# Expert blocks of layer 0 in groups of four, with more tokens gathered, in a two-block transformer kernel

## The chip, the cores and the metric

The kernel runs on one core of a Trainium2 chip, as one program of 61176 instructions in the profiled execution. The metric is the device time of one execution in microseconds (us), the median of several. Before the change three runs took 4265.05, 4275.7 and 4276.56 us, so the median is 4275.7.

## The reference, cut to what matters

The program is two transformer blocks on one sequence. The first block has two layers; each ends with `peer_ffn`, a feed-forward network that picks 128 of 16384 experts for every token (8 heads of 16), each expert a row of `expert_u` and a row of `expert_v`:

```python
D_MODEL, SEQ, CTX_LEN, N_EXPERTS = 1024, 256, 256, 128 * 128

def peer_ffn(h, w_query, sub_keys, expert_u, expert_v):
    ...
    idx = ...    # per token 8 heads x 16 experts
    gate = ...   # their softmax weights
    def block(args):
        tb, ib, gb = args
        act = jax.nn.gelu(jnp.einsum('pkd,pd->pk', expert_u[ib], tb), approximate=False) * gb
        return jnp.einsum('pk,pkd->pd', act, expert_v[ib])
    ...

for i in range(2):              # first block
    ...                         # mixer of layer i: gated delta rule, then windowed attention
    x = x + g2 * peer_ffn(modulate(x, norm2_g[i], sh2, sc2), ...)
    if i == 0:                  # the 256 context tokens go through layer 0 as well
        xc = xc + cg2 * peer_ffn(modulate(xc, norm2_g[i], csh2, csc2), ...)
...                             # second block: mixers, cross attention, mixture of experts
```

So the network of layer 0 sees 512 tokens (256 of the sequence and 256 of the context), that of layer 1 sees 256. The second block ends in a mixture of experts whose weights fill the last third of the profile. All numbers are float32.

## The kernel before, in words

`peer` (line 926) is the network of one layer; `l` is the layer and `n` the number of tokens, T = 256 in layer 1 and T2 = 512 in layer 0. Nearly all of its numbers stand in tables by `n` at lines 38 to 58. `x = FEW[n]` tokens, the last of the 512, take one way, the other `nd = n - x` tokens another. In layer 0, x is 96 and nd 416; in layer 1, x is 0.

**The way of the nd tokens: all experts, masked.** The 16384 experts are 128 blocks of 128. `up(b)` (line 942) computes one block's activations for all nd tokens: the block's u rows come from DRAM (two blocks per transfer of 1 MB into a tile `w`, a ring of three that all weight loads of the program share), are split into a high and a low part of the fp32r type (`wsplit`: ACT writes `whi`, line 347, DVE or POOL writes `wlo`, line 348), and meet the tokens, split in the same way, in 8 x 3 matmuls of nd columns (`mm3`, lines 517 to 519, tile `hps`). ACT applies the gelu into `h`. Then the activations are multiplied with the gate matrix of the block, which is zero where a token didn't pick an expert, split again (`ahi`, `alo`), and multiplied with the block's v rows, 8 x 3 matmuls (tile `dps`, one PSUM bank for each 128 of the 1024 output columns), whose result is scaled by the modulation and added to X, the residual, in SBUF.

The loop (line 1032) takes two blocks a pass, so each PSUM sum covers two blocks, and DVE adds it to X in two instructions (`add`, line 1026, 256 and 160 columns); when no more u blocks are left, one of the 8 adds goes over ACT and POOL (`OFF`). The activations are computed `AHEAD` passes before they are used: 17 in layer 0, in a ring of 18 tiles `hst` of two blocks. 24 further blocks (`SPILL` 12) are computed early too and wait in DRAM (`hd`). The early blocks fill places where TensorE would wait for other engines: 15 (`HEAD`) in the tail of `route`, which picks the experts, the others among the gate matrices.

**The gate matrices** (lines 977 to 1007). For each token two matmuls of one-hot matrices (`oh`, written by DVE, four operations for eight tokens) give the 128 x 128 matrix of its gates (tile `pg`), ACT copies it to a stage, and for each 32 tokens a tile of 2 MB goes to DRAM (`gd`); the loop reads it back by blocks (`gt`). The generator `side`, parts of layer 1's modulation with weights of their own, is stepped in `route` and once in 16 tokens here.

**The way of the x tokens: gathered rows.** `few` (line 1120) is a generator; one step is two tokens. For each token POOL issues two indirect DMAs of 512 KB (line 1134), which fetch the token's 128 u rows (`gu`) and v rows (`gv`), one pair ahead (`LEAD`), from three buffers for u and three for v (`GB`). TensorE broadcasts the token's row to all partitions, in two halves of 512 columns (line 1155, a PSUM tile `bc` each; `few_rows` has cut the row into three bf16 parts), DVE multiplies and sums each half (line 1156), ACT applies the gelu, DVE the gates (`z`), and four fp32 matmuls of 32 result rows (line 1166) sum the v rows into `dn`, which collects 64 tokens before it is transposed (line 1175) and added to X. `tick` (line 1018) steps the generator: each call adds `RATE` to a count, and every 64 make one pair. It is called after each half of the v matmuls, from the fourth pass on (`FIRST`), and after each `up`.

**What sets the order.** A list scheduler of the tile framework puts the instructions of each engine in order; each engine then runs its own in that order. All weight loads stand on SP's queue, the gathers on POOL's, the stores of `gd` and `hd` on ACT's.

## Time and profile before

| of the profiled execution | |
|---|---|
| its own time | 4260.34 us |
| span of the profile | 4258.6 us |
| PE busy | 3796.6 us (89%) |
| PE weight loads (PEld) | 2902.2 us (68%) |
| DVE | 2261.4 us (53%) |
| ACT | 1349.6 us (32%) |
| POOL | 934.0 us (22%) |
| DMA, mean of the span | 241 GB/s |

The profiled execution took 4260.34 us, of which 1.7 lie outside the span; the median of the three runs is 15.4 us above it. The trace gives the stages of layer 0's network by the first and last instruction of their tiles: the tail of `route` from 672 to 760 us, the gate matrices from 760 to 950, the loop from 968 to 2050, with the last `up` at 1862. In layer 1 the gate matrices run from 2349 to 2487 and the loop to about 3040. From about 3290 to the end the mixture of experts loads its weights. Times in the prediction count from the start of the span. Busy shares are of one engine's own instructions, so PE, with matmuls that overlap, may be busy and yet wait; a window's clock column is the share of TensorE's full speed that was granted.

### The profile page before, as it was taken

Reading aid. Unit: us, or ns where it says so; the run is one execution under the profiler, and the core shown is the slowest. Engines: PE = TensorE matmul, PEld = TensorE weight load, DVE = VectorE, ACT = ScalarE, POOL = GpSimd, SP = SyncE. Lnnn points to the kernel's source line nnn. Section 1 sums busy time; section 2 is a strip of 40 time slices with the busy share of each in tenths; the row PEclk is TensorE's granted clock in tenths of the full one; section 3 lists DMA queues with packets and bytes.
Section 4 is the critical chain, followed back from the end, with each engine's and each line's share of the span. In section 5 each row is a group of like instructions: output and inputs, shape, how many; then the busy total and the mean of one; then the engine's idle time right before and its main releaser. Section 6 shows DMA issues by size and latency. Waiting matters only on the chain. (4 is left out here: it accounts for less than half of the span.)

```text
span 4258.6 us, 61176 instructions
## 1 busy us (share of the span) xinstructions
PE 3796.6 (89%) x23913; PEld 2902.2 (68%) x23913; DVE 2261.4 (53%) x5568; ACT 1349.6 (32%) x2363; POOL 934.0 (22%) x671
## 2 busy tenths in 40 slices
PE   7888998999999999999998999999988777777776
PEld 4676767788888888899778999999977211111111
DVE  5777479785665666679669865555575100000000
ACT  4344322443222222233454554444454100000000
POOL 2322235005555555533116000000020000000000
PEclk9889899999999999999999999999999977887788
DMA  5433233877777777755214685656435999999998
GB/s 198 127 109 119 65 139 141 299 265 252 246 242 250 234 242 243 246 189 189 86 60 149 238 307 209 213 207 223 169 130 201 407 416 416 414 416 416 415 416 357
DMA packets 278609, 1028.34 MB, mean 241 GB/s; under 512 B 28208, under 2 KB 151344, under 8 KB 181808
## 3 DMA queue, kind: packets, MB, share of 16 engines
q1 hardware_dynamic: 223824, 847.16, 53.7%
q0 software_dynamic: 28352, 102.77, 7.1%
q10 hardware_dynamic: 26144, 74.49, 4.7%
q8 instruction: 189, 3.10, 0.3%
q14 instruction: 100, 0.82, 0.1%
HBM read 965.72 MB, written 58.03 MB: 240 GB/s over the span
## 5 line engine op out<-in xcount | busy, mean ns | idle before, releaser
L347 ACT CAST whi<-w 128x1024 fp32r<-128x1024 f32 (+2 forms) x651 | 673.6, 1040 | 1152.8 <-PE dps L518 333.5
L348 DVE TENSOR_TENSOR wlo<-w,whi 128x1024 fp32r<-128x1024 f32 (+1 forms) x459 | 552.6, 1209 | 294.5 <-ACT whi L347 293.8
L519 PE MATMUL hps<-hi,wlo 128*128 128x416 f32 (+1 forms) x2048 | 655.8, 320 | 29.1 <-POOL wlo L348 20.3
L517 PE MATMUL hps<-hi,whi 128*128 128x416 f32 (+1 forms) x2048 | 669.0, 327 | 6.5 <-ACT whi L347 6.5
L518 PE MATMUL hps<-lo,whi 128*128 128x416 f32 (+1 forms) x2048 | 657.4, 321 | 0.0
L348 POOL TENSOR_TENSOR wlo<-w,whi 128x1024 fp32r<-128x1024 f32 x192 | 484.4, 2528 | 553.3 <-ACT whi L347 524.5
L1029 DVE SCALAR_TENSOR_TENSOR X<-dps,mod,X 128x256 f32<-128x256 f32 x982 | 377.3, 429 | 281.1 <-PE dps L519 278.6
L2034 PE MATMUL pgu<-mw,xe 128*32 128x512 f32 x1936 | 351.4, 817 | 167.2 <-DMA mw<-in_gu_dram 166.2
L519 PEld LDWEIGHTS hps<-hi,wlo 128*128 128x128 f32 x2048 | 392.1, 192 | 35.9 <-POOL wlo L348 21.9
L517 PEld LDWEIGHTS hps<-hi,whi 128*128 128x128 f32 x2048 | 392.6, 192 | 30.5 <-issue 17.6
L518 PEld LDWEIGHTS hps<-lo,whi 128*128 128x128 f32 x2048 | 392.9, 192 | 2.3
L517 PE MATMUL dps<-ahi,whi 128*128 128x416 f32 x1024 | 371.6, 363 | 1.4 <-DVE X L1029 1.4
L518 PE MATMUL dps<-alo,whi 128*128 128x416 f32 x1024 | 363.7, 355 | 3.7 <-DVE alo L348 3.7
L519 PE MATMUL dps<-ahi,wlo 128*128 128x416 f32 x1024 | 363.0, 355 | 0.0
L2034 PEld LDWEIGHTS pgu<-mw,xe 128*32 128x32 f32 x1936 | 47.0, 123 | 461.2 <-DMA mw<-in_gu_dram 428.7
L517 PE MATMUL ps<-hi,whi 128*128 128x512 f32 (+1 forms) x776 | 287.5, 375 | 22.0 <-ACT hi L347 14.4
L519 PE MATMUL ps<-hi,wlo 128*128 128x512 f32 (+1 forms) x776 | 288.0, 372 | 6.0 <-POOL wlo L348 4.6
L2059 DVE TENSOR_TENSOR hg<-hg,pgu 128x512 f32<-128x512 f32 x16 | 11.0, 688 | 527.6 <-PE pgu L2034 525.8
L519 PE MATMUL acc<-ahi,wlo 128*128 128x256 f32 x1024 | 290.0, 283 | 0.6 <-DVE wlo L348 0.6
L518 PE MATMUL acc<-alo,whi 128*128 128x256 f32 x1024 | 289.9, 283 | 0.5 <-DVE alo L348 0.5
L517 PE MATMUL acc<-ahi,whi 128*128 128x256 f32 x1024 | 289.8, 283 | 0.0
L518 PE MATMUL ps<-lo,whi 128*128 128x512 f32 (+1 forms) x776 | 283.5, 366 | 6.0 <-DVE lo L348 6.0
(565 smaller groups left out, 6314.2 us busy)
## 6 DMA issues: line engine op xcount, KB each, us to landing
mw<-in_gu_dram SPq DMA_DIRECT2D x234, 1024.0 KB, 19.9
w<-in_u_dram SPq DMA_DIRECT2D x128, 1024.0 KB, 6.1
w<-in_v_dram SPq DMA_DIRECT2D x128, 1024.0 KB, 5.0
mw<-in_dn_dram SPq DMA_DIRECT2D x122, 1024.0 KB, 19.9
w<-in_ada_dram SPq DMA_DIRECT2D x48, 1024.0 KB, 5.5
gd<-gst ACTq DMA_DIRECT2D x21, 2048.0 KB, 8.4
gt<-gd SPq DMA_DIRECT2D x32, 832.0 KB, 7.4
w<-in_wq_dram SPq DMA_DIRECT2D x16, 1024.0 KB, 4.8
```

The costliest lines, as they stand in the source:

```text
L347: self.nc.scalar.copy(hi, src)
L348: (lo_eng or self.nc.vector).tensor_tensor(lo, src, hi.bitcast(F32), op=ALU.subtract)
L517: nc.tensor.matmul(ps, whi, xhi, start=first, stop=False)
L518: nc.tensor.matmul(ps, whi, xlo, start=False, stop=False)
L519: nc.tensor.matmul(ps, wlo, xhi, start=False, stop=last)
L1029: nc.vector.scalar_tensor_tensor(X[:, c, ss], ps[:, ss], m[:, 40 + c, s:s + 1], X[:, c, ss], op0=ALU.mult, op1=ALU.add)
L2034: nc.tensor.matmul(ps[half][32 * j:32 * j + 32, :], xe[:, k, e * 32:e * 32 + 32], w[:, 2 * j:2 * j + 2, :], start=k == 0, stop=k == KC - 1)
L2059: nc.vector.tensor_tensor(hg, hg, pgu[1], op=ALU.mult)
```

## The change

- The loop of `peer` takes **four blocks a pass** instead of two (in both layers): a PSUM sum covers four blocks, and X gets half as many additions. The v rows are laid out anew in DRAM, so that a transfer of 1 MB holds four blocks for half of the output columns; a pass takes the columns in two halves. `weigh` (gate product and split of the activations) of the next pass stands behind the first half; the `up`s of a pass, four, stand behind its second half.
- **160 tokens are gathered** in layer 0 instead of 96, so the blocks have 352 columns there instead of 416, and 11 tiles of gate matrices are made instead of 13. 32 pairs are added to the 48.
- `few` is **begun among the gate matrices**: one step for each 32 tokens there (`FEW0`). In the loop `tick` is only called behind each output column chunk of the v matmuls (`RATE` 21, then 8, in place of 19 and 18), eight times a pass, no longer behind an `up`. What is left is stepped at the end of the pass before the last, as it was.
- u and v rows of the gathered tokens **share five buffers** (`GB`) where they had three each; the broadcast row of a token is one PSUM tile of two banks, of which there is one (`BC` 1) where there were two tiles of one bank, and DVE takes the row in one instruction of 1024 elements.
- `side` is used up before the gate matrices begin. `FIRST`, `GE` and `OFF` go: all `up`s among the gate matrices give `wlo` to DVE, and all additions to X are DVE's.

The core of the diff:

```diff
-AHEAD = {T: 17, T2: 3}
+AHEAD = {T: 9, T2: 2}
-SPILL = {T: 12, T2: 18}
+SPILL = {T: 6, T2: 9}
-FEW = {T: 0, T2: 96}
-FIRST = {T: 8, T2: 3}
-RATE = {T: (8, 0), T2: (19, 18)}
+FEW = {T: 0, T2: 160}
+FEW0 = {T: 32, T2: 32}
+RATE = {T: (0, 0), T2: (21, 8)}
-GB = {T: 3, T2: 3}
+GB = {T: 5, T2: 5}
-BC = {T: 1, T2: 2}
-GE = {T: 0, T2: 0}
+BC = {T: 1, T2: 1}
-OFF = {T: 0, T2: 1}
...
-        v = g["peer_v"][l].reshape(NBLK // 2, 2, P, D)
-        o[f"v{l}"] = np.ascontiguousarray(v.transpose(0, 2, 1, 3)).reshape(NBLK // 2, P, 2048)
+        v = g["peer_v"][l].reshape(NBLK // 4, 4, P, 2, 512)
+        o[f"v{l}"] = np.ascontiguousarray(v.transpose(0, 3, 2, 1, 4)).reshape(NBLK // 2, P, 2048)
...
+        for _ in side:
+            pass
         if x:
             rows = self.few_rows(l, n, nd, x, hp, rp, pp, hi, lo)
+        few = self.few(l, X, n, nd, x, hp, pp, *rows, fid, fg) if x else iter(())
...
-            if tok % 16 == 7:
-                next(side, None)
+            if tok % FEW0[n] == FEW0[n] - 1:
+                next(few, None)
             if t % 8 == 7:
                 while (ahead - head + 0.5) * nd < (len(early) - LATE[n] - head) * (tok + 1):
-                    up(early[ahead], (nc.vector, None)[GE[n] * ahead % 4 < GE[n]])
+                    up(early[ahead], nc.vector)
...
+        at = weigh(0)
+        ahead_of(AH - 1)
+        for g in range(NG):
+            first, last = g == 0, g == NG - 1
+            ahi, alo = at
+            for half in range(2):
+                v = self.load(a[f"v{l}"][2 * g + half])
+                vs = [self.wsplit(sp, v[:, i * 1024:(i + 1) * 1024], 1024, tag="v", bufs=VB[n]) for i in range(2)]
+                for c in range(4 * half, 4 * half + 4):
+                    ps = sums[c] if sums else pp.tile([P, 512], F32, tag="sm", name="dps")
+                    for b in range(4):
+                        o = b % 2 * 512 + c % 4 * P
+                        self.mm3(ps[:, :nd], vs[b // 2][0][:, o:o + P], vs[b // 2][1][:, o:o + P], ahi[:, b, :], alo[:, b, :],
+                                 b == 0 and (not sums or first and c % 2 == 0), b == 3 and (not sums or last and c % 2 == 1))
+                    if not sums:
                         add(c, ps)
+                        if last:
+                            self.ssq_add(X, c, sq())
+                    if c == 3 and not last:
+                        at = weigh(g + 1)
                     tick()
...
-            elif g == NBLK // 2 - 2:
+            elif g == NG - 2:
                 for _ in few:
                     pass
...
+            ahead_of(g + AH)
...
-        bc = lambda: pp.tile([P, 512], F32, tag="bc", name="bc", bufs=BC[n])
+        bc = lambda: pp.tile([P, 2, 512], F32, tag="bc", name="bc", bufs=BC[n])
...
-                r = sp.tile([P, D], F32, tag="g" + k, name="g" + k, bufs=GB[n])
+                r = sp.tile([P, D], F32, tag="g", name="g" + k, bufs=GB[n])
...
+                ps = bc()
                 for half in range(2):
-                    s = slice(half * 512, (half + 1) * 512)
-                    ps = bc()
-                    nc.tensor.matmul(ps, sel[:, j:j + 1].to_broadcast([96, P]), h3[:, q, s], start=True, stop=True)
-                    nc.vector.scalar_tensor_tensor(u[:, s], u[:, s], 1.0, ps, op0=ALU.mult, op1=ALU.mult, accum_out=s2[:, k, half:half + 1])
+                    nc.tensor.matmul(ps[:, half], sel[:, j:j + 1].to_broadcast([96, P]), h3[:, q, half * 512:(half + 1) * 512], start=True, stop=True)
+                nc.vector.scalar_tensor_tensor(u, u, 1.0, ps.rearrange("p h c -> p (h c)"), op0=ALU.mult, op1=ALU.mult, accum_out=act[:, k:k + 1])
```

A group is a pass with four blocks, here and below. Three places show what the scheduler makes of it. A row is an instruction by its line, operation, output and inputs; `x2` is twice in a row.

On POOL in the loop of layer 0, before (L1134 are the gathers, L348 the low part of a u block, L1038 the product with the gates):

```order
L1134 DMA gu<-in_ur_dram,fid 128x1024 x2
L1134 DMA gv<-in_vr_dram,fid 128x1024 x2
L348 TENSOR_TENSOR wlo<-w,whi 128x1024 x2
L1134 DMA gu<-in_ur_dram,fid 128x1024 x2
L1038 TENSOR_TENSOR hst<-hst,gt 128x832
```

The same place with the change, where the gathers are L1143, the low parts L347 and the product L1042:

```order
L1143 DMA gu<-in_ur_dram,fid 128x1024
L347 TENSOR_TENSOR wlo<-w,whi 128x1024 x2
L1042 TENSOR_TENSOR hst<-hst,gt 128x704
L347 TENSOR_TENSOR wlo<-w,whi 128x1024 x2
L1042 TENSOR_TENSOR hst<-hst,gt 128x704
L1143 DMA gv<-in_vr_dram,fid 128x1024
L1143 DMA gu<-in_ur_dram,fid 128x1024
```

Before, the gathers of a pair stood in twos, spread over the other work; now v and u gathers alternate in a row of eleven, and four low parts and two products stand between two such rows.

On PE, where the last pair of gathered tokens of layer 0 is summed, before (L1155 are the broadcasts, L1166 the sums, L1175 the transposes, L517 to L519 the block matmuls):

```order
L518 MATMUL dps<-alo,whi 128x416
L1166 MATMUL dn<-gv,z 32x512 x4
L519 MATMUL dps<-ahi,wlo 128x416
L517 MATMUL dps<-ahi,whi 128x416
L518 MATMUL dps<-alo,whi 128x416
L519 MATMUL dps<-ahi,wlo 128x416
L1175 MATMUL bc<-cst,y 128x64 x8
```

With the change (L1163, L1172, L1181, and L516 to L518 for the block matmuls):

```order
L1163 MATMUL bc<-h_6921,sel 128x512
L1172 MATMUL dn<-gv,z 32x512 x4
L1163 LDWEIGHTS sel
L1163 MATMUL bc<-h_6921,sel 128x512
L1163 LDWEIGHTS sel
L1163 MATMUL bc<-h_6921,sel 128x512
L1172 MATMUL dn<-gv,z 32x512 x4
L1181 MATMUL bc<-cst,y 128x64 x8
L516 MATMUL dps<-ahi,whi 128x352
```

Before, block matmuls stand between the steps of the last pair, and more than 1,000 of them follow it; now the steps of the last pairs stand one behind the other, and 48 block matmuls follow.

On DVE among the gate matrices, before (L987 to L990 write the one-hot matrices):

```order
L988 TENSOR_TENSOR oh_7583<-i_6881,i1T 128x1024
L987 TENSOR_TENSOR oh_7582<-i_6881,i2T 128x1024
L989 TENSOR_TENSOR oh_7584<-oh_7583,g_4912 128x1024
L990 TENSOR_TENSOR oh_7583<-oh_7583,g_4912 128x1024
L348 TENSOR_TENSOR wlo<-w,whi 128x1024 x2
```

With the change (L990 to L993 now, L1164 the product of a gathered row):

```order
L992 TENSOR_TENSOR oh_7827<-oh_7826,g_4912 128x1024
L347 TENSOR_TENSOR wlo<-w,whi 128x1024
L993 TENSOR_TENSOR oh_7826<-oh_7826,g_4912 128x1024
L1164 SCALAR_TENSOR_TENSOR gu,act<-gu,bc 128x1024
L990 TENSOR_TENSOR oh_7884<-i_7015,i2T 128x1024
L991 TENSOR_TENSOR oh_7885<-i_7015,i1T 128x1024
L1164 SCALAR_TENSOR_TENSOR gu,act<-gu,bc 128x1024
```

The products of gathered rows now stand among the one-hot operations; before there were none in this stage.

## Rows read from the trace of the kernel before

**Rows 1.** The page, section 2: busy tenths in 40 slices, and GB/s.
```profile
PE   7888998999999999999998999999988777777776
...
GB/s 198 127 109 119 65 139 141 299 265 252 246 242 250 234 242 243 246 189 189 86 60 149 238 307 209 213 207 223 169 130 201 407 416 416 414 416 416 415 416 357
```

**Rows 2.** Windows by stage: us, busy PE, PEld, DVE, ACT, POOL, PEclk, DMA share, GB/s.
```profile
672.00:760.00 88.00, 69.99 (x367) 66.84 (x366) 82.88 (x188) 26.24 (x36) 47.71 (x16) 0.88 0.38 136
760.00:968.00 208.00, 198.20 (x1610) 172.74 (x1608) 163.85 (x238) 101.03 (x167) 6.18 (x6) 1.00 0.79 294
...
1100.00:1800.00 700.00, 698.36 (x3735) 618.14 (x3734) 430.33 (x1045) 202.24 (x278) 385.61 (x261) 1.00 0.72 242
...
1862.00:2050.00 188.00, 188.00 (x998) 186.25 (x996) 165.59 (x345) 69.44 (x104) 59.78 (x40) 1.00 0.57 184
```

**Rows 3.** Windows with block matmuls alone, 416 columns, then layer 1's 256.
```profile
1900.00:2000.00 100.00, 100.00 (x531) 99.08 (x531) 91.21 (x188) 38.12 (x56) 34.69 (x22) 1.00 0.64 207
2700.00:2800.00 100.00, 100.00 (x836) 100.00 (x835) 52.30 (x52) 45.32 (x61) 0.00 (x0) 1.00 0.56 198
```

**Rows 4.** PE's timeline over one pair: start, us, engine, line, operation.
```profile
1300.74 0.61 PE L1155 MATMUL bc<-h,sel 96*128 96x512 bf16 x2
...
1303.18 0.35 PE L519 MATMUL dps<-ahi,wlo 128*128 128x416 f32 x1
...
1304.69 0.35 PE L518 MATMUL dps<-alo,whi 128*128 128x416 f32 x1
1304.97 1.07 PE L1166 MATMUL dn<-gv,z 128*32 128x512 f32 x8
...
1306.45 0.35 PE L518 MATMUL dps<-alo,whi 128*128 128x416 f32 x1
```

**Rows 5.** PE's timeline in the gate stage.
```profile
873.33 1.09 PE L994 MATMUL pg<-oh,oh 128*128 128x128 f16 x16
874.22 0.44 PE L519 MATMUL hps<-hi,wlo 128*128 128x416 f32 x1
```

**Rows 6.** Tile gv: form xcount: ns min/median/max, first to last us; then landing.
```profile
L1166 PE MATMUL dn<-gv,z x384: 592/604/618, 1015.9 to 1845.8; 128*32 128x512 f32 x192
L1134 POOL DMA_INDIRECT gv<-in_vr_dram,fid x96: 933/937/1586, 960.7 to 1830.2; - x96
...
DMA to landing us min/median/max: 4.3/5.9/10.2
```

**Rows 7.** Lines by form on DVE, 672 to 2050 us, columns of section 5.
```profile
L1029 DVE SCALAR_TENSOR_TENSOR X<-dps,mod,X 128x256 f32<-128x256 f32 x488 | 235.3, 482 | 280.0 <-PE dps L519 277.5
...
L1156 DVE SCALAR_TENSOR_TENSOR gu<-gu,bc 128x512 f32<-128x512 f32 x192 | 122.6, 684 | 77.5 <-PE bc L1155 73.5 <-DMA gu<-in_ur_dram,fid 3.7
...
L988 DVE TENSOR_TENSOR oh<-i,i1T 128x1024 f16<-128x1024 f16 x52 | 35.8, 689 | 22.4 <-PE pg L994 22.3
```

**Rows 8.** The same on POOL.
```profile
L348 POOL TENSOR_TENSOR wlo<-w,whi 128x1024 fp32r<-128x1024 f32 x98 | 254.5, 2598 | 275.4 <-ACT whi L347 275.2
```

**Rows 9.** Timelines of POOL and of DVE about one gather.
```profile
1129.10 1.48 POOL L1134 DMA_INDIRECT gu<-in_ur_dram,fid  x1 [0.33 <-DVE gu L1156]
...
1128.75 1.02 DVE L348 TENSOR_TENSOR alo<-hst,ahi 128x832 fp32r<-128x832 f32 x1
...
1129.75 1.22 DVE L348 TENSOR_TENSOR wlo<-w,whi 128x1024 fp32r<-128x1024 f32 x1
```

**Rows 10.** PE's timeline behind its long wait, in brackets idle and releaser.
```profile
745.24 0.71 PE L519 MATMUL hps<-hi,wlo 128*128 128x416 f32 x1 [13.74 <-POOL wlo L348]
...
746.10 0.55 PE L518 MATMUL hps<-lo,whi 128*128 128x416 f32 x1
746.45 0.55 PE L519 MATMUL hps<-hi,wlo 128*128 128x416 f32 x1
```

**Rows 11.** The page, section 6: DMA issues, KB each, us to landing.
```profile
w<-in_u_dram SPq DMA_DIRECT2D x128, 1024.0 KB, 6.1
...
gd<-gst ACTq DMA_DIRECT2D x21, 2048.0 KB, 8.4
```

More of the change, by code (lines that the diff above doesn't have):

```diff
@@ L959, in up @@
                 nc.scalar.dma_start(hd[b0 - kept], h)
-        early = [*range(2 * AH), *range(kept, NBLK)]
+        early = [*range(4 * (AH - 1)), *range(kept, NBLK)]
         es1 = ExitStack()
@@ new lines, in weigh @@
+        def weigh(g):
+            gt = sp.tile([P, nd // TG, 4, TG], F32, tag="gt", name="gt")
+            nc.sync.dma_start(gt, gdv[:, :, 4 * g:4 * g + 4, :])
+            ahi, alo = (sp.tile([P, 4, nd], F32R, tag=t, name=t) for t in ("ahi", "alo"))
+            for i in range(2):
+                h, b = hs.pop(2 * g + i), slice(2 * i, 2 * i + 2)
+                hv = h.rearrange("p b (g t) -> p b g t", t=TG)
+                (nc.vector if n == T else nc.gpsimd).tensor_tensor(hv, hv, gt[:, :, b, :].rearrange("p g b t -> p b g t"), op=ALU.mult)
+                self.split(ahi[:, b], alo[:, b], h)
+            return ahi, alo
@@ new lines, in ahead_of @@
+        def ahead_of(g):
+            if g >= NG:
+                return
+            if 4 * g < kept:
+                for b in range(4):
+                    up(4 * g + b, nc.vector if n == T else None)
+                return
+            for p in (2 * g, 2 * g + 1):
+                hs[p] = hp.tile([P, 2, nd], F32, tag="hst", name="hst", bufs=NH)
+                nc.sync.dma_start(hs[p], hd[2 * p - kept:2 * p - kept + 2].rearrange("b p t -> p b t"))
+        at = weigh(0)
+        ahead_of(AH - 1)
```

66 lines of the change are left out of this document (14 added, 52 removed).

## The prediction, made before the run

> **What bounds the kernel now.** I read the page first: its slices say where TensorE is the limit. From the second slice of 40 to the 31st PE stands at 8 or 9 tenths; in the last nine it falls to 7 and 6, and in eight of them 407 to 416 GB/s flow [rows 1]. Those nine belong to the second block and aren't touched; they move as a whole with what happens ahead of them. Then the windows by stage of layer 0 [rows 2]. The tail of the routing (672 to 760 us) has PE busy 70.0 of 88 us at a granted clock of 0.88, and DVE 82.9: DVE sets the end there. The gate matrices (760 to 968) have PE 198.2 and DVE 163.9 of 208. In the loop over the blocks (1100 to 1800) PE is busy 698.4 of 700 us at a full clock, DVE 430, POOL 386, the DMA engines 72% at 242 GB/s; in the loop's end (1862 to 2050) PE has 188.0 of 188. Here only TensorE's work counts. Layer 1's loop is the same in kind, 100.0 of 100 [rows 3].
>
> **What one matmul costs.** In a window with nothing on PE but block matmuls of 416 columns there are 531 in 100 us, or 188.3 ns each; with 256 columns 836, or 119.6 ns [rows 3]. So a column costs (188.3 - 119.6) / 160 = 0.43 ns, and 352 columns come to 160.8 ns: 27.5 ns less.
>
> **The change on TensorE, part by part.**
> - Block matmuls: 128 blocks x 24 for the first half and the same for the second, 6144 x 27.5 ns = -169.0 us. The 336 that now stand in the tail of the routing win nothing, since PE waits for DVE there [rows 2]: +9.2.
> - Gate matrices of 64 tokens fewer, two matmuls each: 16 take from 873.33 to 874.22, 56 ns each [rows 5]: 128 x 56 ns = -7.2.
> - 64 more gathered tokens, 32 pairs. Four broadcast matmuls push the row of block matmuls from 1300.74 to 1303.18, 2.44 us in which eight of 188 ns run: 0.93 us. The sum over experts (dn) pushes the third matmul after 1304.69 to 1306.45, 1.76 less 3 x 0.188: 1.20 us. A pair costs 2.13 us [rows 4]: +68.2.
> - 16 more matmuls that prepare rows, and one more batch of 8 transposes: +3, estimated from the 56 to 188 ns of the others.
>
> The sum on the path is -95.8 us. Half the additions to X go away (L1029, 482 ns for 256 columns [rows 7]); they lie under PE, which is full, so I count nothing, and if that cover went, it would be a gain. The dot product of a gathered row becomes one instruction of 1024 elements. The trace has 512 in 684 ns [rows 7]; at the 0.8 ns per element between 256 and 512 that gives 1.1 us, and two of the old ones 1.4; I take 1.2, and it stays under PE. It reads a broadcast tile of two banks, of which there is one in place of two: PE's next two broadcasts wait for DVE. Between them stand 11 to 18 block matmuls (1.8 to 2.9 us), so I count nothing; without that cover it would be up to 1.2 us for each of the loop's 68 pairs. In layer 1 the blocks are 256 columns as before and PE is full: nothing, with 5 us to either side.
>
> **The waits it adds.** All of them concern the gathers, whose five buffers are now shared by u and v rows.
> - The loop. The fetches of a pair stand on POOL one behind the other, and the v row of one token waits until the sum of the pair before has read its buffer. From one sum's start to the next at least its own 1.07 us [rows 4], 0.1 to wake POOL, the 5.9 from issue to landing [rows 6] and 0.1 must pass: 7.2 us. The order of PE gives the spacing. Before, pairs are 15 to 20 us apart. Now they are bunched into the second-half matmuls; in three groups of four blocks the starts are 24.1, 6.5, 9.2, 22.7, 8.7, 21.9, 10.1 and 6.5 us apart by the prices above (6.5 is 27 block matmuls, four broadcasts and the sum). Two of eight are too close, by 0.75 us. In the 21 groups before the kept blocks run out that is 14 x 0.75 = +10.5. The landing was between 4.3 and 10.2 us; at 4.3 the wait is 0, at 10.2 a spacing needs 11.5 and the loop loses 117 us. I take the median, from the same transfer at 242 GB/s [rows 2]; a group now asks for 10.4 MB in some 37 us, 280. Behind the waiting fetch POOL has the split of the next u block, 2.6 us [rows 8], which the block's third matmul needs: once in three groups it may come 0.7 us late, within the bounds.
> - The last four pairs come in one burst behind the 31st of 32 groups, with 34 block matmuls among them and 48 behind. Their starts are 5.1, 4.5, 2.1 and 1.7 us apart on PE, and each needs 7.2: 28.8 - 13.4 = 15.4, and 1.6 until the first transpose: +17 (bounds 5.6 to 11.5 per pair: 10 to 34). Before, the last sum ran at 1845.8 [rows 6], 200 us ahead of the end. PE starves there; after an idle 13.74 us the trace shows matmuls at 0.35 us instead of 0.19, the lower level of the clock, 1.2 GHz [rows 10]. For the 48 that is 0 to 7 us: +3.
> - The gate stage. PE gets 12 pairs (+25.6), loses the 7.2, and its 720 first-half matmuls are 19.8 shorter, so its work stays as it is. DVE loses 8 sets of four one-hot operations of 0.69 us [rows 7], some 20 us, and gets some 31 from the pairs: about 175 of 208, still under PE. The first two pairs are 3.4 us apart and lack 4. The loads for layer 1's modulation, spread over the stage before, now stand at its front, 9 of 1 MB, each needing 2.5 us at 416 GB/s while DVE supplies 88 tokens in 30 us: 8 us. Together +12, with 0 and 60 as ends, the upper one from the DMA (below).
>
> Net: -95.8 + 10.5 + 17 + 3 + 12 = -53 us. The profiled execution took 4260.3 us (span 4258.6), 15.4 below the median of 4275.7, which lies in runs of 4265 to 4277; against the median this gives **4223 us**.
>
> **Two rules weighed.** Issuing a gather takes POOL 0.94 us [rows 6]; one that began while DVE subtracted two SBUF tiles took 1.48 and ended 0.8 us after it, while DVE's next such subtraction ran inside the gather for its usual 1.22 us [rows 9]. So DVE holds up a gather and a gather doesn't hold up DVE, and 48 gathers in the gate stage cost POOL some 25 us, which has little else to do there. The Trainium skill ("SBUF — State Buffer", "SBUF: two separate sides") says that DVE and GpSimd share a port pair under an exclusive lock, and that whichever starts first blocks the other fully. By that rule gathers would stall DVE too; the trace agrees with one half of it. The Trainium skill (same page, "A bandwidth-pool intuition that's wrong") gives a core about 358 GB/s from HBM; by that the 78 MB of the gate stage, below, would take 218 us, 10 more than the stage has now. The slices at 416 GB/s speak against it [rows 1].
>
> **Rivals.**
> - The gathers land late: slower, 10%. In the bunched stretches two pairs, the v loads and the next u loads meet. If a gather takes 10.2 us, its largest row [rows 6], the loop loses 117, the end 37: -95.8 + 117 + 37 + 12 = +70, 4346 us. It decides from a landing of 8.3 us on, where the waits add up to the gain. For it speaks the 5.9 at a mean of 242 GB/s; against it, that 416 can flow.
> - The gate stage becomes a DMA stage: no change, 11%. Its transfers are 11 gate tiles of 2 MB and 15 u loads of 1 MB [rows 11], 9 loads as large for the modulation, 48 gathers of 0.5 MB and 5 MB of spilled blocks, 78 MB. At the stage's present 294 GB/s [rows 2] that is 265 us against 208: 57 in place of my 12, 4268 us. At the 416 of the last slices it is 187, and hidden.
> - Gathers hold up DVE in the gate stage: 48 x 0.94 = 45 us make DVE 220 of 208 us, some 15 us more than forecast: 4238 us, 4%.
> - Everything is hidden, because POOL runs ahead and landings are short: -96, 4180 us, 18%.
>
> **How the numbers follow.** My forecast, with waits of 15 to 75 us, has 53%; 4% is left for other ways of being faster. 0.3% (13 us) is about what a measurement of this kernel tells from no change. Faster by more: 0.53 + 0.18 + 0.04 + 0.04, rounded to 0.78; within it 0.11; slower 0.11, with a point for what I don't see. The range goes from the case without waits and the runs' own spread (4175) to past the DMA case (4285). It leaves out most of the late gathers and a little below.
>
> **What would show it.** Block matmuls about 161 ns apart in layer 0, some 622 in 100 us of a window that holds nothing else. The gate stage about 220 us long, the loop behind it some 65 us shorter. The sum over experts preceded by PE waits for DMA (gv) or DVE (z) of about 1 us in the loop and 3 to 6 us each in the last burst. Layer 1's loop unchanged. I am wrong if matmuls of 352 columns aren't cheaper by 27 ns, if gathers land later than 8 us, or if the gate stage is over 230 us.

## The result: slower, where faster was forecast

The changed kernel takes 4333.1 us (median of four runs, 4318.2 to 4340.5) where the kernel before took 4270.4 beside it (four runs, 4257.6 to 4276.6): a ratio of 1.0146, interval 1.0107 to 1.0186. The prediction was 4223, its range 4175 to 4285; it was wrong in sign, and the time lies near that of a rival with a chance of 10%. The profiled execution took 4328.5, its span 4326.8.

One correction to the description of the kernel before: it gives some values of layer 0 from layer 1's column of the tables. In layer 0 `AHEAD` is 3 (a ring of four tiles), `SPILL` 18 (36 blocks in DRAM) and `HEAD` 13; with the change they are 2, 9 groups (36 blocks) and 13. The prediction's numbers went by the trace and the order.

By first and last instruction of their tiles the stages are, in us:

| stage | before | after | difference |
|---|---|---|---|
| start to the first gate matmul | 759.5 | 757.5 | -2.0 |
| gate matrices, to the first dps | 208.9 | 260.3 | +51.4 |
| layer 0's loop, first to last dps | 1084.3 | 1099.5 | +15.2 |
| from there to the end | 2206.0 | 2209.5 | +3.5 |

Two more blocks are computed ahead of the loop than before, 44 (40 early and four by `ahead_of(AH - 1)`) against 42: 48 matmuls of 161 ns, or 7.7 us, left the loop, and 33 of them, 5.3 us, lie in the gate stage. So without that the gate stage is 46 us longer and the loop 23; forecast were 12 longer and 65 shorter. (The expectation of gates3, below, takes 15 us for these 5.)

The windows of the changed kernel, with the columns of [rows 2]:

```profile
757.00:968.00 211.00, 175.26 (x1453) 138.10 (x1454) 164.76 (x260) 86.28 (x152) 50.99 (x46) 0.91 0.90 344
968.00:1018.00 50.00, 40.35 (x223) 37.07 (x222) 18.34 (x17) 17.86 (x27) 24.44 (x13) 0.90 0.79 282
...
1100.00:1800.00 700.00, 643.80 (x3774) 559.05 (x3773) 307.89 (x596) 195.71 (x280) 392.95 (x277) 0.97 0.72 251
1800.00:1891.00 91.00, 83.11 (x477) 71.52 (x476) 39.89 (x79) 23.66 (x36) 50.06 (x36) 0.94 0.71 250
...
2050.00:2117.00 67.00, 54.13 (x273) 37.19 (x271) 34.00 (x72) 12.19 (x21) 23.93 (x24) 0.82 0.60 206
...
1905.00:1950.00 45.00, 45.00 (x280) 40.18 (x279) 36.08 (x70) 14.77 (x19) 18.18 (x16) 1.00 0.81 287
```

In the loop, where PE was busy 698 of 700 us [rows 2], it is now 644, and the granted clock is 0.97 where it was 1.00. The last row, a stretch of block matmuls alone, has 280 in 45 us: 160.7 ns each, as forecast. So the matmuls got as cheap as they should, and PE waits. Its waits in the loop (line waited for; us in total, times, longest):

```profile
PE bc L1163 <- DVE gu L1164: 34.5, 15, 3.1
PE dn L1172 <- DVE z L1167: 19.4, 14, 2.5
PE dn L1172 <- DMA gv<-in_vr_dram,fid: 9.7, 6, 3.3
PE hps L518 <- POOL wlo L347: 4.8, 7, 1.1
```

All but the last are steps of the gathered pairs. Over the whole loop PE idles 84.1 us (before: 9.3). The clock takes some 41 more: (1 - clock) times the length, as 0.03 x 700 = 21 of it from 1100 to 1800. By the trace 5 of them fall on time in which PE idles anyway, so it costs some 36. Without both the loop would take 980 us; the forecast's 1019, less its 30.5 us of waits and clock and less the 7.7 us that moved, is 981. The work was priced about right; what went wrong in the loop is waits and the clock behind them.

### The profile page after: what moved, and what is told of

It is laid out like the page before. It is cut to its first block, busy times and chain, and to the rows that moved or that the text cites. A ratio compares the mean times of both kernels' runs of the same rounds, so it can differ in the third digit from the quotient of the medians.

```text
span 4326.8 us, 61005 instructions
## 1 busy us (share of the span) xinstructions
PE 3733.2 (86%) x24193; PEld 2795.6 (65%) x24193; DVE 2100.6 (49%) x4992; ACT 1325.0 (31%) x2342; POOL 1021.6 (24%) x780
## 5 line engine op out<-in xcount | busy, mean ns | idle before, releaser
L347 DVE TENSOR_TENSOR wlo<-w,whi 128x1024 fp32r<-128x1024 f32 (+2 forms) x457 | 551.6, 1217 | 390.5 <-ACT whi L346 379.3
L516 PE MATMUL hps<-hi,whi 128*128 128x352 f32 (+1 forms) x2048 | 636.9, 311 | 18.1 <-ACT whi L346 16.2
L518 PE MATMUL hps<-hi,wlo 128*128 128x352 f32 (+1 forms) x2048 | 632.5, 309 | 22.1 <-POOL wlo L347 12.5
L517 PE MATMUL hps<-lo,whi 128*128 128x352 f32 (+1 forms) x2048 | 628.5, 307 | 0.0
L347 POOL TENSOR_TENSOR wlo<-w,whi 128x1024 fp32r<-128x1024 f32 x194 | 472.4, 2445 | 368.9 <-ACT whi L346 347.6
L518 PEld LDWEIGHTS hps<-hi,wlo 128*128 128x128 f32 x2048 | 394.0, 192 | 42.2 <-POOL wlo L347 16.8
L516 PEld LDWEIGHTS hps<-hi,whi 128*128 128x128 f32 x2048 | 395.0, 193 | 31.0 <-ACT whi L346 19.8
L517 PEld LDWEIGHTS hps<-lo,whi 128*128 128x128 f32 x2048 | 394.7, 193 | 8.6 <-issue 7.5
L516 PE MATMUL dps<-ahi,whi 128*128 128x352 f32 x1024 | 359.7, 351 | 3.3 <-DVE X L1030 3.3
L518 PE MATMUL dps<-ahi,wlo 128*128 128x352 f32 x1024 | 345.5, 337 | 0.0
L517 PE MATMUL dps<-alo,whi 128*128 128x352 f32 x1024 | 340.6, 333 | 0.0
L516 PE MATMUL ps<-hi,whi 128*128 128x512 f32 (+1 forms) x776 | 286.9, 374 | 21.0 <-ACT hi L346 12.6
L518 PE MATMUL ps<-hi,wlo 128*128 128x512 f32 (+1 forms) x776 | 287.1, 371 | 5.7 <-POOL wlo L347 4.3
L516 PE MATMUL acc<-ahi,whi 128*128 128x256 f32 x1024 | 289.9, 283 | 0.0
L517 PE MATMUL acc<-alo,whi 128*128 128x256 f32 x1024 | 289.9, 283 | 0.0
L518 PE MATMUL acc<-ahi,wlo 128*128 128x256 f32 x1024 | 289.9, 283 | 0.0
L517 PE MATMUL ps<-lo,whi 128*128 128x512 f32 (+1 forms) x776 | 282.6, 365 | 7.6 <-DVE lo L347 7.6
L2078 PE MATMUL py<-mw,hT 128*32 128x512 f32 x976 | 220.4, 668 | 55.6 <-DMA mw<-in_dn_dram 44.7
L1143 POOL DMA_INDIRECT gv<-in_vr_dram,fid x160 | 172.3, 1077 | 402.7 <-DVE gu L1164 242.6
```

Source lines behind the costliest of these rows:

```text
L347: (lo_eng or self.nc.vector).tensor_tensor(lo, src, hi.bitcast(F32), op=ALU.subtract)
L516: nc.tensor.matmul(ps, whi, xhi, start=first, stop=False)
L517: nc.tensor.matmul(ps, whi, xlo, start=False, stop=False)
L518: nc.tensor.matmul(ps, wlo, xhi, start=False, stop=last)
L1143: nc.gpsimd.indirect_dma_start(out=r, out_offset=None, in_=a[f"{k}r{l}"], in_offset=bass.IndirectOffsetOnAxis(ap=fid[:, t:t + 1], axis=0))
L2078: nc.tensor.matmul(py[dh][32 * j:32 * j + 32, :], hT[:, s, 32 * j:32 * j + 32], w[:, 4 * j2 + 2 * dh:4 * j2 + 2 * dh + 2, :], start=s == 0 ...
```

## How a pair waits

One wait followed back to its start. On POOL (start, us, engine, line, operation; in brackets idle before it and releaser):

```profile
1287.23 0.94 POOL L1143 DMA_INDIRECT gu<-in_ur_dram,fid  x1 [0.30 <-PE hps L518]
1288.23 2.40 POOL L347 TENSOR_TENSOR wlo<-w,whi 128x1024 fp32r<-128x1024 f32 x1
1292.07 2.40 POOL L347 TENSOR_TENSOR wlo<-w,whi 128x1024 fp32r<-128x1024 f32 x1 [1.44 <-ACT whi L346]
1294.43 1.71 POOL L1042 TENSOR_TENSOR hst<-hst,gt 128x704 f32<-128x704 f32 x1
1298.04 4.76 POOL L347 TENSOR_TENSOR wlo<-w,whi 128x1024 fp32r<-128x1024 f32 x2 [1.90 <-ACT whi L346]
1302.75 1.70 POOL L1042 TENSOR_TENSOR hst<-hst,gt 128x704 f32<-128x704 f32 x1
1308.22 0.98 POOL L1143 DMA_INDIRECT gv<-in_vr_dram,fid  x1 [3.76 <-DVE gu L1164]
```

Then on ACT, DVE and PE:

```profile
1302.40 0.61 PE L1163 MATMUL bc<-h,sel 96*128 96x512 bf16 x2
1304.49 0.78 ACT L346 CAST ahi<-hst 128x704 fp32r<-128x704 f32 x1 [4.50 <-POOL hst L1042]
1305.30 0.89 DVE L347 TENSOR_TENSOR alo<-hst,ahi 128x704 fp32r<-128x704 f32 x1 [3.92 <-ACT ahi L346]
1306.73 1.21 DVE L1164 SCALAR_TENSOR_TENSOR gu<-gu,bc 128x1024 f32<-128x1024 f32 x1
1308.00 0.59 PE L1163 MATMUL bc<-h,sel 96*128 96x512 bf16 x2 [3.06 <-DVE gu L1164]
```

PE broadcasts a token's row at 1302.40. Its product with the gathered row needs only that broadcast and the row, and all rows fetched so far had landed by 1294; DVE stands idle. But on DVE the product stands behind `alo`, the low part of the weighed activations. That waits for ACT's high part `ahi` (3.92 us), `ahi` waits for POOL's product with the gates (4.50 us), and that product stands behind POOL's low parts of the u blocks. So the row's product starts at 1306.73 only, and until it is done the one broadcast tile isn't free for the next token: PE idles 3.06 us. No gather has a part in this wait.

The same queue stands ahead of the gathers too: between two of them POOL has four low parts and two products, 13 us of work and 3.3 of waiting for ACT. What a late gather costs looks like this:

```profile
1311.89 1.06 PE L1172 MATMUL dn<-gv,z 128*32 128x512 f32 x8
1313.24 1.13 POOL L1143 DMA_INDIRECT gv<-in_vr_dram,fid  x1 [2.17 <-PE dn L1172]
1322.70 1.16 PE L1172 MATMUL dn<-gv,z 128*32 128x512 f32 x6 [3.35 <-DMA gv<-in_vr_dram,fid]
```

The sum at 1311.89 frees a buffer, the fetch behind it lands 9.4 us later, and the next sum, begun at 1318.30, waits 3.35 us for it. That is the wait that the prediction had in mind, with a longer landing.

Every wait of PE from the first `dps` to the last `up`, followed back in this way from releaser to releaser (us, and times in brackets; "by POOL's product" is the first kind; what is left over, under 1 us a run, is none of these):

| run | all | by POOL's product | by a landing | by POOL's low part itself |
|---|---|---|---|---|
| the change | 68.7 | 46.9 (21) | 16.9 (15) | 4.8 (7) |
| uuvv | 62.1 | 47.4 (21) | 9.7 (11) | 4.8 (7) |
| spread | 63.9 | 60.0 (26) | 0 | 3.0 (5) |
| gb6 | 49.0 | 48.1 (21) | 0 | 0.7 (1) |
| dve | 28.6 | 0 | 28.6 (17) | 0 |
| uuvvdve | 20.1 | 0 | 20.1 (11) | 0 |
| gb6wlo | 11.4 | 11.4 (13) | 0 | 0 |
| gb6dve, tail | 0 | 0 | 0 | 0 |

The runs are those of the next section. The prediction looked for waits in the gathers alone; two thirds of the waits came by the first way.

## The experiments

Seventeen kernels ran, each with runs of the kernel before beside it (its median 4263.5 to 4270.4). Gates, loop and idle are the stages of the table above and PE's idle time in the loop, of the profiled execution.

| run | median | ratio to before, interval | gates | loop | idle |
|---|---|---|---|---|---|
| the change | 4333.1 | 1.0146, 1.0107 to 1.0186 | 260.3 | 1099.5 | 84.1 |
| uuvv | 4336.6 | 1.0167, 1.0132 to 1.0201 | 261.8 | 1096.5 | 77.2 |
| spread | 4331.8 | 1.0153, 1.0123 to 1.0183 | 263.1 | 1088.8 | 82.2 |
| gb6 | 4294.0 | 1.0075, 1.0045 to 1.0105 | 257.3 | 1058.6 | 63.2 |
| dve | 4284.9 | 1.0054, 1.0036 to 1.0073 | 254.1 | 1053.4 | 54.6 |
| uuvvdve | 4273.8 | 1.0021, 1.0004 to 1.0038 | 252.5 | 1045.6 | 43.0 |
| gb6prod | 4282.2 | 1.0049, 1.0028 to 1.0070 | 253.9 | 1057.6 | 72.0 |
| gb6wlo | 4231.8 | 0.9914, 0.9888 to 0.9940 | 256.5 | 996.8 | 23.3 |
| gb6dve | 4228.8 | 0.9918, 0.9895 to 0.9942 | 252.7 | 1000.2 | 24.2 |
| tail | 4209.5 | 0.9879, 0.9863 to 0.9896 | 253.7 | 985.2 | 14.0 |
| few192 | 4237.9 | 0.9946, 0.9928 to 0.9965 | 241.7 | 1024.9 | 68.4 |
| side | 4352.0 | 1.0197, 1.0165 to 1.0229 | 274.5 | 1101.2 | 88.6 |
| rowsearly | 4337.5 | 1.0167, 1.0136 to 1.0198 | 257.6 | 1107.5 | 89.0 |
| nofew0 | 4329.1 | 1.0142, 1.0112 to 1.0172 | 251.4 | 1101.1 | 79.5 |
| gates2 | 4232.2 | 0.9930, 0.9913 to 0.9946 | 271.6 | 984.8 | 13.1 |
| gates3 | 4243.6 | 0.9958, 0.9942 to 0.9975 | 242.8 | 1020.3 | 29.1 |
| adadn0 | 4204.3 | 0.9867, 0.9834 to 0.9901 | 248.9 | 988.9 | 16.1 |
| side6 | 4227.3 | 0.9913, 0.9887 to 0.9939 | 203.5 | 988.8 | 17.2 |

### The buffers and their order

Six shared buffers (the SBUF for the sixth comes from tiles that share their place):

```diff
-GB = {T: 5, T2: 5}
+GB = {T: 5, T2: 6}
...
```

> The change with six shared buffers instead of five (room made by letting spilled blocks and the transposed sums share tiles, one z, and three shared tiles in the routing). Theory A: the second u row takes the buffer of the pair's first u row and no longer waits for the sum; as in the run with u, u, v, v or a little better, 4265 to 4290 us. Theory B: no change, 4320 to 4340 us.

39 us better, all of it in the loop (41 us shorter). Five buffers cost that much, and the waits for landings are gone. But 63 us of idle time stay: A is at work and isn't all. (The 11.6 us from sum to sum, 1265.34 to 1276.94, that the expectations go by, held no wait: PE had block matmuls all the while, and the u row fetched at 1268.68 belongs to the pair after.)

Five buffers in another order, a pair fetched as u, u, v, v:

```diff
-            for k in ("u", "v"):
+            for k, t in (("u", t), ("u", t + 1), ("v", t), ("v", t + 1)):
...
```

> The change, but a pair's gathers are issued u, u, v, v instead of u, v, u, v, so that of the five shared buffers only the second v row waits for the sum of the pair before; bytes and buffers stay. Theory A (the loop loses its time in the round trip of a pair: the second u row waits for the sum of the pair before, and behind its landing still come the product, the gelu, the gates and the sum, 11.6 us from sum to sum in the trace): the round trip falls to some 8 us, PE's waits for DVE gu and z, 34.5 and 19.4 us between 1018 and 1890, fall by more than half, the loop gets 40 to 60 us shorter with the clock that returns, 4275 to 4295 us. Theory B (gathers land late because the DMA engines are shared by more work): landings don't care for the order, 4320 to 4340 us.

Nothing came of it (4336.6), against A as I had put it: of PE's waits up to the last `up` only those for `z` fall, from 19.4 to 12.6 us; those at `bc` stay, 34.7, since they come by POOL's product and not by a gather. It was tried again with POOL free (uuvvdve, below).

The same pairs spread evenly, with steps behind each `up` as well:

```diff
-RATE = {T: (0, 0), T2: (21, 8)}
+RATE = {T: (0, 0), T2: (14, 8)}
...
+                    step()
...
-            ahead_of(g + AH)
+            ahead_of(g + AH, tick)
```

> The change, with steps of gathered pairs also behind each up (rate 14 over 12 calls a group instead of 21 over 8), so as many pairs per group but spaced 9 to 18 us apart instead of 6.5 to 24. Theory A: with a round trip of 11.6 us only some spacings are still short, by about 2 us each, so two thirds of the loop's 64 us of waits and of the lower clock go, 4275 to 4295 us, with the burst at the end as it is. Theory B: the same bytes in the same time, 4315 to 4340 us.

Nothing again: 82 us of idle time, though by PE's order the pairs stand 9 to 18 us apart. Spreading did away with the waits for landings, with five buffers, and the waits by POOL's product grew by as much. One of them, of 2.6 us for a pair's gates, takes a way over ACT; its rows on POOL and ACT:

```profile
1231.83 4.76 POOL L347 TENSOR_TENSOR wlo<-w,whi 128x1024 fp32r<-128x1024 f32 x2 [1.90 <-ACT whi L346]
1236.55 1.67 POOL L1042 TENSOR_TENSOR hst<-hst,gt 128x704 f32<-128x704 f32 x1
...
1238.25 0.78 ACT L346 CAST ahi<-hst 128x704 fp32r<-128x704 f32 x1 [4.46 <-POOL hst L1042]
1238.93 0.20 ACT L1166 ACTIVATE act<-act 128x2 f32<-128x2 f32 x1
```

The pair's product was done at 1236.1, but its gelu (L1166) ran at 1238.93, behind a split on ACT that waited 4.46 us for POOL's product, which stood behind POOL's low parts. The expectations tell two ways apart in which POOL holds up a pair: its gathers (C1) and, by way of ACT, its gelu (C2). The way over ACT's split and DVE's `alo`, shown above, is a third, which no expectation names and which most of the waits took.

### POOL's other work

All of the loop's other POOL work to DVE, with five buffers and with six:

```diff
-                (nc.vector if n == T else nc.gpsimd).tensor_tensor(hv, hv, gt[:, :, b, :].rearrange("p g b t -> p b g t"), op=ALU.mult)
+                nc.vector.tensor_tensor(hv, hv, gt[:, :, b, :].rearrange("p g b t -> p b g t"), op=ALU.mult)
...
-                    up(4 * g + b, nc.vector if n == T else None)
+                    up(4 * g + b, nc.vector)
```

> The change, with the loop's other POOL work (the product with the gates and the low part of the u blocks, some 300 us from 1018 to 2118) given to DVE, so that POOL has only gathers; five buffers as in the change. Theory A (round trip through five shared buffers alone): the round trip stays, the loop stays within 15 us, 4315 to 4340 us. Theory C (the gathers stand in POOL's queue behind batches of four low parts and two products, some 13 us a group, which themselves wait for ACT): the gathers are issued as soon as a buffer is free, PE's 64 us of waits in the loop fall by half or more, 4270 to 4300 us; the waits on landings stay.

> Six buffers and the loop's other POOL work on DVE. If A and C are both at work, the loop's waits before the last burst nearly vanish (under 15 us from 1018 to 1890) and the time is 4250 to 4275 us. If A alone: as with six buffers, 4285 to 4300 us. If DVE becomes the bound, the waits name DVE's low part of u and the time is over 4300.

48 us from POOL's work alone, 39 from the sixth buffer alone, 104 from both, more than their sum: each alone leaves the other's wait in place, as the table of waits shows (dve has landings only, gb6 POOL's product only). With both, the loop looks as in the kernel before, at the full clock; its window as long as blocks are kept in SBUF:

```profile
1011.00:1775.00 764.00, 764.00 (x4705) 675.21 (x4704) 513.58 (x865) 243.45 (x349) 224.42 (x218) 1.00 0.81 287
```

PE is busy in all 764 us. The gathers land later than in the changed kernel; the tile `gu` of gb6dve and of the change:

```profile
DMA to landing us min/median/max: 4.0/7.2/24.4
```

```profile
DMA to landing us min/median/max: 4.1/6.2/25.3
```

So theory B, that the loop is slow because landings are late, falls: with a median of 7.2 us they cost PE nothing here, with 6.2 they cost 16.9 us in the change.

Then each half of POOL's work, with six buffers:

> Six buffers, and of POOL's other work in the loop only the product with the gates on DVE; the low parts of the u blocks stay on POOL. Theory C1 (what counts is that gathers stand in POOL's queue behind the low parts, 10 of the 13 us a group): little changes against the 4294 us with six buffers, 4275 to 4295 us. Theory C2 (what counts is that ACT's split of the weighed activations waits for POOL's product, which stands behind POOL's low parts, and that the gelu of a gathered pair stands behind that split on ACT: in the trace of the change ACT waits 181 us for that product in the loop): ACT no longer waits for POOL there, 4230 to 4255 us.

> Six buffers, and only the low parts of the u blocks on DVE; the product stays on POOL. C1: the batch ahead of the gathers falls from 13 to 3.5 us, 4235 to 4255 us. C2: the product has only gathers ahead of it, but ACT still waits for POOL's 1.8 us products, 4240 to 4265 us. Less than this run alone, the pair of it and the run with the product on DVE tells the two apart.

The low parts on DVE bring all (loop 996.8), though ACT still waits for POOL's products, for 2.8 us at most where it was 4.8 in the change; ACT's and PE's waits from 1018 to 1790 us:

```profile
ACT ahi L346 <- POOL hst L1042: 105.1, 42, 2.8
...
PE bc L1163 <- DVE gu L1164: 9.9, 8, 1.3
PE dn L1172 <- DVE z L1167: 1.5, 5, 0.3
```

The product on DVE brings the loop nothing (1057.6 against 1058.6), and ACT waits for POOL no longer. But that run doesn't speak for C1, for on DVE the product met the low parts again. POOL and DVE in gb6prod:

```profile
1072.25 2.99 DVE L1167 TENSOR_TENSOR z<-act,fg 128x2 f32<-128x2 f32 x1 [0.61 <-ACT act L1165]
1072.87 2.35 POOL L347 TENSOR_TENSOR wlo<-w,whi 128x1024 fp32r<-128x1024 f32 x1
...
1080.18 2.41 POOL L347 TENSOR_TENSOR wlo<-w,whi 128x1024 fp32r<-128x1024 f32 x1 [1.32 <-ACT whi L346]
1080.50 2.84 DVE L1042 TENSOR_TENSOR hst<-hst,gt 128x704 f32<-128x704 f32 x1 [5.25 <-ACT hst L957]
```

DVE's product, 0.88 us in gb6dve, takes 2.8 beside a low part on POOL and ends 0.8 us after it; seven times the gates `z`, else 0.16 us, take 3.0. PE's waits in this run, 44.7 us up to the last `up`, are of these two kinds but for 0.7.

So POOL's low parts are the cause, as gb6 against gb6wlo shows (4294.0 and 4231.8). That the way is the third one is read from the traces: with six buffers and the low parts on POOL, 48.1 of 49.0 us of waits come by POOL's product, and none by a gather. That low parts ahead of the gathers cost anything of their own (C1) no run shows; dve, without them, has more waits for landings than the change.

> Five buffers in the order u, u, v, v, with the loop's other POOL work on DVE; to be held against 4285 us for u, v, u, v with the same. If the order failed to help before only because POOL's and ACT's queues hid it, only the second v row now waits for a sum and 25 us or more of the 55 us of PE's idle time go, 4240 to 4262 us. If five buffers are too few in any order, 4275 to 4295 us.

With POOL free, the order u, u, v, v brings 11 us over u, v, u, v (4273.8 against 4284.9, with intervals that touch), just under the range expected if five buffers are too few in any order. They are too few in both orders while the pairs are bunched; what the order is worth stays small and not settled. Spread pairs with POOL free and five buffers weren't run.

### The end of the loop, and more gathered tokens

The product on DVE only while blocks are kept, and rates that leave no pair for the end:

```diff
-RATE = {T: (0, 0), T2: (21, 8)}
+RATE = {T: (0, 0), T2: (21, 13)}
...
+                (nc.vector if n == T or 4 * g < kept else nc.gpsimd).tensor_tensor(hv, hv, ...
```

> Six buffers, POOL's low parts on DVE, the product with the gates on DVE only while blocks are kept and on POOL for the spilled ones, and rates 21 and 13 so that no pair is left for a burst at the end. The run with six buffers and DVE idled 24 us and had clocks of 0.93 and 0.80 behind 1850 us, where DVE waits 21 us for reloaded blocks in front of the additions to X, and the last pairs come in one burst. If both are the causes, the loop falls from 1000 to some 975 us, 4200 to 4212 us. If the burst only moves its landings ahead and the reloads set the pace on POOL as well, 4220 to 4235 us.

4209.5 us, 19 under the run without it, 15 of it in the loop. This and adadn0 below gained most of all runs, 1.2 and 1.3% of the kernel before. Two edits went in together here; what each brought isn't shown.

192 tokens (`FEW` 192, rates 27 and 14) on top of it:

> As tail, with 192 gathered tokens (320 columns; rates 27 and 14). By the prices of the prediction, which the trace bore out for the block matmuls (160 ns at 352 columns), 32 columns fewer are worth 6144 x 13.75 ns = 84 us, 16 pairs more cost 34 us: 50 us less on PE, 4150 to 4165 us if no wait comes back. If the pairs, now some 10 us apart in the loop, meet the round trip of six buffers (about 8 us and POOL's issue) or the DMA engines (81% busy in the loop with six buffers and DVE), the gain is eaten: 4195 to 4230 us.

The gain is more than eaten, 28 us slower than tail: PE's waits for `z` (34.6 us) and for `bc` (30.8) are back, and where the trace has the landing of a row whose product DVE waited for, the product starts with it. With sums as little as 4.5 us apart, six buffers are too few again. No run has a seventh.

### The gate stage

Five edits, each on the change or on tail: the modulation stepped once in 16 tokens again (side); the rows' preparation ahead of the early `up`s (rowsearly); no pair in this stage (nofew0, `FEW0` 1024, rates 24 and 14); the first two together on tail (gates2); all three (gates3).

> The change, with layer 1's modulation spread over the gate stage again (one step in 16 tokens) instead of used up ahead of it. Theory G1 (the stage from 757 to 1018 us is bound by its bytes, 89 MB): the same bytes lie in it, less than 8 us better, 4325 to 4340 us. Theory G2 (the stage loses its time at its front: the modulation matmuls wait for their loads, 9 us, then the preparation of the gathered rows stands alone on PE from 796 to 825 us, waits 9 us for DVE, and 30 us pass with 50 to 70 GB/s): the preparation moves back to the tail of the routing, the stage gets 20 to 35 us shorter, 4295 to 4315 us.

> The change, with the preparation of the gathered tokens' rows put ahead of the early ups in the tail of the routing instead of behind layer 1's modulation. Theory G2 (the hole of 25 us at 800 to 830 us with 50 us of idle DMA engines comes from this preparation standing alone on PE): the hole goes, the stage from the first gate matmul to the first dps falls from 260 to 230 or 240 us, 4300 to 4315 us. Theory G1 (bytes): the stage is bound by 89 MB and gets at most 10 us shorter, 4320 to 4340 us.

> The change, with no pairs begun among the gate matrices: all 80 in the loop (rates 24 and 14 instead of 21 and 8, so none is left for a burst at the end). The 12 pairs' own work moves, some 26 us of PE. Theory G1: the gate stage loses its 24 MB of gathers and falls from 260 to 215 us or less, the loop grows by 26 us and the waits of 12 more pairs (0.8 us each), and loses the last burst's 13 us; 4290 to 4315 us. Theory G2: the stage falls only by the pairs' own work, to some 235, and the time stays, 4315 to 4340 us.

> As the run named tail, with the modulation spread over the gate stage again and the rows' preparation ahead of the early ups. Alone, each left the stage from the first gate matmul to the first dps at 258 to 275 us. If the two holes at its front cover each other (one filled, the other takes its place), together they bring 15 to 30 us, 4180 to 4195 us. If the stage is set by bytes, it stays above 250 us and the time is that of tail or 10 us worse.

> As gates2, and no pairs among the gate matrices (rates 24 and 14), so that the stage holds what it held before the change, with 64 tokens fewer. If pairs, modulation and preparation together make the stage long, it falls to some 205 to 215 us (209 before, of which 15 us of ups that now stand ahead of the loop are new); the loop gets 26 us of pairs back: net 10 to 25 us under gates2. If it stays near 250, the cause is none of the three but the single broadcast tile that modulation and pairs share, or the ups' own order.

None brought the stage back to 209 us. Spreading the modulation made it 14 to 18 us longer, against both theories; the early preparation brought nothing: its matmuls ran from 767 to 791 us instead of 796 to 822, still behind the first gate matmul. Leaving the pairs out brought 9 us where G1 gave 45, but it was half the dose: PE reached 5 of the 11 pairs before the first `dps` all the same, and of the stage's bytes 12 MB went, not 24. The stage in before, the change, nofew0 and side6 (below), with the columns of [rows 2]:

```profile
759.50:968.30 208.80, 199.00 (x1617) 173.47 (x1618) 164.42 (x240) 101.20 (x167) 6.48 (x6) 1.00 0.79 294
757.50:1017.80 260.30, 215.41 (x1673) 174.95 (x1674) 182.60 (x275) 104.01 (x177) 74.93 (x58) 0.91 0.88 332
765.80:1017.20 251.40, 204.50 (x1604) 173.65 (x1605) 170.48 (x250) 103.14 (x172) 52.56 (x36) 0.92 0.79 297
825.80:1029.30 203.50, 187.42 (x1545) 159.77 (x1546) 176.66 (x270) 96.09 (x165) 65.39 (x50) 0.98 0.96 364
```

That is 61, 86, 75 and 74 MB. Nofew0 and side6 move the same bytes in 251 and 204 us, so bytes alone don't set the length; and neither G1 nor G2 holds alone.

Then the modulation's sum in the bank of `dn`, and on top of it the early preparation and twice as many of its steps in the routing:

```diff
-{"ada": ("bc", BC[n])}
+{"ada": ("dn", 1)}
...
-SIDE = 3
+SIDE = 6
```

> As the run named tail, with layer 1's modulation summed in the PSUM bank of the gathered sums (dn, unused until the first pair) instead of the one broadcast tile. Theory G3 (with one broadcast tile a part of the modulation holds it over eight loads, so the rows' preparation can't start before the modulation is used up; spreading, moving it and leaving pairs out all left the stage long for that reason): the preparation moves into the tail of the routing, the hole at 800 to 830 us goes, and the stage falls from 254 to 230 to 240 us, 4185 to 4197 us. If the stage is long for its loads alone: no change, 4203 to 4217 us.

> As adadn0, with the preparation ahead of the early ups and twice as many steps of the modulation in the routing (SIDE 6), where DMA engines and PE have room (136 GB/s and 64 of 85 us in its tail). Theory G3 with the drain at the front: the 10 loads at the stage's front, PE's 9 us of waits for them and the low clock of 0.78 behind them go too; the stage falls to 215 to 225 us, 4170 to 4185 us. If the routing is held up by the loads, its start of the gate matmuls moves from 763 us by as much as the stage gains: 4195 to 4215 us.

With the other bank the preparation runs from 550 to 779 us, so the broadcast tile did hold it back; but half of its 32 matmuls still come behind the first gate matmul (755 us). That brings the stage only 5 us, and the whole agrees with tail within the intervals: G3 holds for little. In side6 all of the preparation and all of the modulation's loads lie ahead of the stage, which takes 203.5 us, with clock 1.00 in its window:

```profile
672.00:826.00 154.00, 116.58 (x626) 97.22 (x624) 108.79 (x397) 36.56 (x50) 73.46 (x32) 0.86 0.40 146
826.00:984.00 158.00, 147.75 (x1322) 122.76 (x1319) 153.89 (x246) 77.94 (x139) 59.02 (x45) 1.00 0.98 377
```

But the first gate matmul now comes at 825.8 us instead of 755.0, and the whole is 23 us slower. So the loads and the rest of the preparation together go with some 45 us of the stage's length (248.9 less 203.5), and ahead of it they cost more than that. Which of the two it is wasn't run apart. That these loads lie in the stage can't be all of it: the kernel before has nine of them there (the change six), stepped once in 16 tokens, and takes 209 us. How much of it is DMA, and how much PE's waits and its clock (0.91 in the change, 1.00 before), is not settled.

## Why the prediction was wrong

- **What bounds the kernel, and a matmul's cost**: right. 160.8 ns forecast, 160.7 measured; the gathered row's product 1.2 forecast, 1.21 measured; layer 1 unchanged (3.5 us over all behind layer 0's loop).
- **The loop**: the step that failed is "All of them concern the gathers", of the waits that the change adds. It said of the product of a gathered row that "it stays under PE", and counted nothing for the one broadcast tile, with 11 to 18 block matmuls (1.8 to 2.9 us) as cover. That took the tile as held for the product's 1.2 us; but the product stands on DVE behind a split that waits for POOL. PE waits 34.5 us at the tile up to the last `up`, up to 3.1 each, and 46.9 of all 68.7 us come by POOL's product behind POOL's low parts. The gathers themselves were sized nearly right: +10.5 forecast, 16.9 us of waits for landings found, and the sixth buffer brought 41 us of loop, clock included. The late low part, 0.7 us once in three groups, came as it said: seven times, 0.6 to 1.1. Waits and clock took 120 us of the loop where 30.5 stood in the sum.
- **The clock**: the sum had +3, for the last burst. After waits of 1 to 3 us throughout the loop the matmuls are 0.29 us apart in places instead of 0.16, the lower level of 1.2 GHz; the loop's mean clock of 0.96 cost some 36 us beside the waits. In gb6dve it is 1.00 as long as blocks are kept, without the waits.
- **The last burst**: +17 forecast. PE idles 13 us in its window, mostly until rows land, and the clock of 0.82 costs at most 12: right in kind and size.
- **The gate stage**: +12, against 51.4. The prediction took its 720 first-half matmuls as if as many had stood there before; 687 had, which makes 5 us. The other 34 are a term mis-sized, and which one stays open: PE's idle time rose from 10 to 45 us and its clock fell from 1.00 to 0.91. The waits that the trace names are for the modulation's loads (9.0 us), for ACT's split of u blocks (9.7) and, in the preparation of the rows, for DVE (8.7). The 8 us for the loads, held against DVE's supply, are not shown wrong by themselves.
- **The rivals**: "The gathers land late" came near the time (4346) with the wrong mechanism: landings have medians of 6.2 and 6.5 us, far from its 8.3. That the time came out close to it is luck. "Everything is hidden" gave 4180; with the waits removed the loop of tail came to 985 us, near the 980 without any, so that rival's loop is to be had, by other means than the change. The DMA rival's 265 us for the gate stage came near too (260, with 86 MB at 332 GB/s), but 12 MB fewer brought 9 us only. The rival that was true, POOL's low parts as what holds up the pairs' other steps, wasn't among them.

## What to carry to other kernels

When a step of one chain (here a gathered row's product) shares an engine with another chain (here the split of the activations), read what stands *ahead* of the step in that engine's queue, and what that in turn waits for; follow it over all engines before you call a step hidden. Cover counted in matmuls holds only if the step starts when its own inputs are there. When a trace names the last engine that a wait ended on, go on back from there: PE's waits here name DVE's product, and the cause stands on POOL, two engines further. And count the clock: 84 us of idle time came with 36 more by the clock in the changed kernel, though in nofew0 (79.5 idle, mean clock 0.99) with 15, so there is no fixed share.

## What the runs showed of the hardware that I had not expected

The low part of 128 x 1024 elements takes POOL twice what it takes DVE (the groups by line of the changed kernel and of gb6dve, 1018 to 1790 us):

```profile
L347 POOL TENSOR_TENSOR wlo<-w,whi 128x1024 fp32r<-128x1024 f32 x73 | 174.5, 2400 | 57.9 <-ACT whi L346 57.2
```

```profile
L347 DVE TENSOR_TENSOR wlo<-w,whi 128x1024 fp32r<-128x1024 f32 x168 | 205.4, 1222 | 192.0 <-ACT whi L346 190.2
```

2400 against 1222 ns. The Trainium skill ("GPSIMD Engine Reference", "4.1 Engine selection") says of additions and products of a tile that GPSIMD takes about twice as long for two inputs; the trace agrees. The Trainium skill ("PSUM — Partial Sum Buffer", "Engine vs sequencer instructions") calls the queues of ScalarE, VectorE and GpSimdE strictly first in, first out; the rows of DVE at 1305 to 1307 us and of ACT at 1238 show what that costs a product and a gelu behind a waiting instruction.

The lock between DVE and POOL that the prediction weighed shows both sides between their arithmetic: DVE's product takes 2.8 us for 0.88 beside POOL's low parts (gb6prod), and POOL's product 2.3 for 1.7 in gb6wlo, where it runs beside DVE's subtractions. For a gather it stayed one-sided. In gb6dve, where POOL has only gathers in the loop's first part, a gather of 0.94 us takes 1.50 beside a subtraction on DVE, and the subtraction its usual 1.22:

```profile
1320.55 1.50 POOL L1143 DMA_INDIRECT gu<-in_ur_dram,fid  x1 [0.30 <-issue]
...
1320.01 1.22 DVE L347 TENSOR_TENSOR wlo<-w,whi 128x1024 fp32r<-128x1024 f32 x1 [0.64 <-ACT whi L346]
```
